# Each visit's first cast ahead of the finished visit's copies, in a grouped SwiGLU up-projection

## The chip, the cores and the metric

The kernel runs on one core of a Trainium2 chip. The metric is device time in microseconds, the median of the runs shown. A separate profiled execution gives the trace. TensorE does the matrix products; ScalarE (ACT in the profile), VectorE (DVE) and GpSimd (POOL) do the rest; SyncE (SP) issues nearly all transfers between the chip's memory and the on-chip memory. Matmul results are added up in PSUM banks.

## The reference

One decoder layer in float32, for 256 tokens and a model width of 2048:

```python
mod = (silu(c) @ w_ada + b_ada).reshape(b, 9, 2048)
h = rms_norm(x, norm_ffn1) * (1 + mod[:, 1]) + mod[:, 0]
x = x + 0.5 * mod[:, 2] * swiglu(h, w_ffn1_gu, w_ffn1_down)     # 2048 -> 2 x 5632 -> 2048
h = rms_norm(x, norm_mix) * (1 + mod[:, 4]) + mod[:, 3]
x = x + mod[:, 5] * token_mixing(h, w_in, ...)                  # retention beside windowed attention
h = rms_norm(x, norm_ffn2) * (1 + mod[:, 7]) + mod[:, 6]
x = x + 0.5 * mod[:, 8] * swiglu(h, w_ffn2_gu, w_ffn2_down)
return rms_norm(x, norm_final)

def swiglu(h, w_gu, w_down):
    gate, up = split(h @ w_gu, 2)
    return (silu(gate) * up) @ w_down
```

The change concerns the first `h @ w_ffn1_gu` alone.

## The kernel before

**Products.** Every float32 operand of a large product is split in two: a rounded high part, made by a cast on ScalarE (`split`, L374, tile `wh` for weights), and the low part, the difference, made by a subtraction on VectorE (L376, tile `wl`). Three products stand for one: high x high, low activation x high, high x low (`products`, L359). A *piece* is two blocks of 128 rows of a weight by 512 columns; for the 256 tokens (two banks) it takes 12 matmuls. Tiles `wh` and `wl` have three buffers each, so pieces can be made at most three ahead. Weights land in tiles `raw`, four buffers of 1 MB (four blocks by 512 columns).

**The grouped start.** The first up-projection begins while the conditioning vectors `mod` are still being computed from `w_ada` on VectorE (`ada_pass`, L219; its rows are loaded at L214). The 16 blocks of h therefore come in four groups of 2, 4, 6 and 4 blocks (`bounds`). For the first 8 pairs of column chunks, 16 chunks n of 512 columns (even n: gate, odd n: up), each group goes over all chunks: a *visit* is one chunk with one group's blocks, so 1, 2, 3 and 2 pieces. The order of the chunks is turned round from group to group, so that the last two chunks of a group (`stay`) are the first two of the next and keep their banks. In between, a chunk's partial sums leave PSUM: `to_parts` (L1170) copies both banks out to on-chip memory on ScalarE. PSUM has four accumulation banks here (`acc_bank`), two visits' worth. When a visit of the second or third group starts on a chunk with sums, ScalarE copies them back into its new banks (L1143), and the matmuls go on from there. The last two chunks of the third group start empty. In the fourth group (`final`) all do, and `swiglu_up` adds the kept sums on VectorE (L704, L705), then takes Silu on ScalarE (L707) and the product on VectorE (L708).

**Turning the result.** What `swiglu_up` makes is transposed by DMA: two copies on ScalarE into planes (`apart`, L534), a transpose that SyncE issues from a tile `flat` into a tile `back` (L539; `back` has four buffers), and two copies on ScalarE from `back` to their place (`together`, L550), which free the buffer. These steps are spread over later visits: `turn_step` advances every open chain (`later`) by a step, once per visit in the fourth group and once per load in the plain up-projection (`ffn_up`, `gemm_part`, loads at L350) that follows for the other three chunk pairs.

**What sets the order.** SyncE issues its transfers in the order in which the program writes them down; one that must wait, for a free buffer or for data, holds the ones behind it. On the compute engines a planner orders instructions at build time, from estimated times; at run time each engine goes through its list in that order. `tc.issue_after(ins)` ties the instructions of its block behind `ins` in the list of that instruction's engine. `cast[-1]` and `low[-1]` are the cast and the subtraction written down last. In the kernel before, the loop over the visits writes down, for one visit: its copies in, behind the cast written last; its loads; for each piece a cast, a subtraction and 12 matmuls, and in the later groups a `tick` that may write down loads and passes of conditioning rows; then in the fourth group `turn_step`; in the other groups the work for the next group's blocks of h (`coming`, with its rows); then the copies out, or `swiglu_up`.

Of the kernel before, what the change touches and what calls it, by code (L numbers as in the profile page):

```python
# [20 lines left out]
DFF = 5632  # L21
NT = S // P
KD = D // P
KF = DFF // P
CH = 512
# [52 lines left out]
def layer_kernel(  # L78
# [614 lines left out]

    def swiglu_up(banks_g, banks_u, tiles, ci, parts=None, by_dma=False):

        k0 = ci * KB
        dest = tiles[k0 // KD].rearrange("p (k s) -> p k s", s=S)
        kk = k0 % KD
        work = []
        for t in range(NT):  # L700
            s = t512()
            g, u = banks_g[t], banks_u[t]
            if parts is not None:
                nc.vector.tensor_add(s, g, parts[0][t])  # L704
# [12 lines left out]
        if work:  # L717
            turns.append(later(work))

    def ffn_up(held, w, tiles, first, bg=None, turned=(), ahead=None):  # L720
        for ci in range(first, DFF // CH):
            bg = bg or gemm(held, w, [ci * CH])[0]
            bu = gemm(held, w, [DFF + ci * CH], ahead=ahead)[0]
            swiglu_up(bg, bu, tiles, ci, by_dma=ci in turned)
            bg = ahead = None

# [326 lines left out]

    banks, moved, unlinted = {}, set(), set()
    for n, one_bank in zip(firsts, (acc_bank, side_bank)):
# [75 lines left out]

    def visit(n, ks, ends, ticks=False, ends_all=False):
        starts = n not in banks
        seeded = starts and n in moved and not ends_all
        if starts:
            banks[n] = [acc_bank() for _ in range(NT)]
        if starts:
            unlinted.discard(n)
        if seeded:
            unlinted.add(n)  # L1140
            for b, p in zip(banks[n], part_of(n)):
                with tc.issue_after(cast[-1]):
                    nc.scalar.copy(b, p)  # L1143
        raw_of = [(load_blocks(n, part), part) for part in (ks[:KB], ks[KB:]) if part]
# [4 lines left out]
        ]  # L1149
        for raw, part in pieces:  # L1150
            a, b = part[0] - ks[0], part[-1] + 1 - ks[0]
            hl = slice(part[0], part[-1] + 1)
            wh, wl = split(wsp, "w", raw[:, : len(part), :], CH)
            products(
# [4 lines left out]
                wl,  # L1159
                starts and a == 0 and not seeded,  # L1160
                b == len(ks) and ends,
                seeded=n in unlinted,
            )
            if ticks:
                tick()

    def to_parts(n):
# [16 lines left out]
    for g, ks in enumerate(groups):  # L1184
# [11 lines left out]
        for i, n in enumerate(order):  # L1196
            if g == 0 and n in firsts:
                continue
            visit(n, ks, n not in stay, g == len(groups) - 2 or final and i < 12, final or (g == len(groups) - 2 and n in stay))
            if final:  # L1200
                turn_step()
# [18 lines left out]
            elif n % 2:  # L1220
# [487 lines left out]
```

## Time and profile before

| | |
|---|---|
| median of 3 runs | 2363.13 us (2362.26 to 2363.86) |
| profiled execution, its own time | 2364.78 us |
| its span, first to last instruction | 2363.0 us |
| instructions | 28368 |
| mean granted TensorE clock | 0.999 of full speed |
| casts at L374 | 792, 1053 ns each |
| subtractions at L376 | 792, 1223 ns each |
| copies out at L1170 | 82 |
| copies in at L1143 | 52 |
| bytes read from memory | 597.16 MB, 254 GB/s over the span |

How to read the profile: times are microseconds from the first instruction of the program. PE is TensorE's matmul, PEld its weight load, which runs beside it; SPq stands for SyncE's issuing of transfers. A group or a timeline row names line, engine, operation and tiles (out<-in), a count and durations, and then the idle time of that engine just before and what ended it. A wait is put down to whatever came last. Shares of the DMA are means over 16 engines. A TensorE that is busy is not always at full rate: matmuls overlap, so the steady rate is read from the number of them in a stretch. The granted clock is a share of full speed.

### The profile page before, as it was taken

To read this page: it belongs to the slowest core of one execution; us is meant where nothing else is said; L and a number is where in the kernel's file an instruction comes from. 1 tells how busy PE (TensorE), PEld (TensorE's weight loads), DVE (VectorE), ACT (ScalarE), POOL (GpSimd) and SP (SyncE) were. 2 spreads that over 40 slices of the span, in tenths; PEclk is the share of its full clock that TensorE was granted. 3 is DMA by queue.
4 is the path that set the end of the run, shared out by engine and by line. 5 is a ranking of instruction groups with operands and counts; after the bars stand their busy time and mean duration, and the time that the engine had idled before them with its cause. 6 is when DMAs were issued, how large, how long until landed. Compare 5 with 4: busy or idle time off the path is not lost.

```text
span 2363.0 us, 28368 instructions
## 1 busy us (share of the span) xinstructions
PE 2338.4 (99%) x10447; PEld 1919.6 (81%) x10447; DVE 1670.4 (71%) x2576; ACT 1375.4 (58%) x1907; POOL 9.2 (0%) x21
## 2 busy tenths in 40 slices
PE   8999999999999999999999999999999999999998
PEld 5888788788888888778888888888888888888887
DVE  7788787778867768976777876677655555545656
ACT  6766568555556568775556554465455455455544
POOL 0000000000000000000000000000000000000000
PEclk9999999999999999999999999999999999999999
DMA  9988879988776788866688787754767777776553
GB/s 381 367 336 333 331 247 330 375 308 318 273 255 238 274 282 234 266 213 245 267 287 292 295 286 296 289 205 179 246 237 257 248 240 258 226 232 204 194 196 125
DMA packets 194765, 629.98 MB, mean 267 GB/s; under 512 B 117249, under 2 KB 117633, under 8 KB 124097
## 3 DMA queue, kind: packets, MB, share of 16 engines
q1 hardware_dynamic: 192130, 617.14, 74.5%
q0 software_dynamic: 1600, 9.83, 1.1%
q8 instruction: 82, 1.34, 0.2%
q10 hardware_dynamic: 896, 1.19, 0.1%
q14 instruction: 57, 0.47, 0.1%
HBM read 597.16 MB, written 4.22 MB: 254 GB/s over the span
## 4 chain that ended last, share of the span: by engine, by line
PE 95%; DMA 3%; ACT 1%; DVE 1%; issue 0%; SPq 0%; DVEq 0%; ACTq 0%
PE pa L359 93%; DMA raw<-in_w_ffn_gu_dram 2%; PE ps L1393 0%; ACT wh L374 0%; DMA slot<-in_w_ada_dram 0%; PE pd L1309 0%; DMA x_sb<-in_x_dram 0%; PE ps L359 0%; ACT slot L1170 0%; PE ps L893 0%; PE pd L1491 0%; PE ps L1309 0%; DVE slot L219 0%; PE pd L1492 0%; PE pd L1478 0%
## 5 line engine op out<-in xcount | busy, mean ns | idle before, releaser
L376 DVE TENSOR_TENSOR wl<-raw,wh 128x1024 fp32r<-128x1024 f32 x792 | 961.7, 1223 | 535.5 <-ACT wh L374 469.7
L374 ACT CAST wh<-raw 128x1024 fp32r<-128x1024 f32 x792 | 828.8, 1053 | 805.1 <-PE pa L359 753.7
L359 PE MATMUL pa<-wh,hh 128*128 128x512 f32 x2184 | 595.4, 392 | 7.6 <-ACT wh L374 6.9
L359 PE MATMUL pa<-wh,hl 128*128 128x512 f32 x2184 | 590.6, 390 | 0.0
L359 PE MATMUL pa<-wl,hh 128*128 128x512 f32 x2184 | 586.6, 390 | 0.0
L359 PEld LDWEIGHTS pa<-wh,hh 128*128 128x128 f32 x2184 | 407.1, 188 | 97.6 <-ACT wh L374 11.8
L359 PEld LDWEIGHTS pa<-wh,hl 128*128 128x128 f32 x2184 | 410.5, 188 | 86.3 <-issue 0.4
L359 PEld LDWEIGHTS pa<-wl,hh 128*128 128x128 f32 x2184 | 410.2, 188 | 86.4 <-issue 0.8
L359 PE MATMUL pa<-wh,a 128*128 128x512 f32 x1824 | 452.4, 389 | 0.0
L359 PEld LDWEIGHTS pa<-wh,a 128*128 128x128 f32 x1824 | 341.7, 188 | 70.5
L359 PE MATMUL pa<-wl,a 128*128 128x512 f32 x912 | 245.2, 389 | 0.0
L219 DVE CUSTOM_DVE_ANT_0 slot<-slot,cact 128x512 f32<-128x512 f32 (+2 forms) x292 | 222.2, 811 | 13.3 <-DMA slot<-in_w_ada_dram 12.9
L359 PEld LDWEIGHTS pa<-wl,a 128*128 128x128 f32 x912 | 171.1, 188 | 35.4
L550 ACT COPY slot<-back 128x512 uint16<-128x512 uint16 x156 | 104.0, 766 | 0.0
L219 DVE CUSTOM_DVE_ANT_0 rows_x<-rows_x,cact 128x512 f32<-128x512 f32 x124 | 78.8, 688 | 19.8 <-DMA rows_x<-in_w_ada_dram 19.6
L534 ACT COPY flat<-t 128x512 uint16<-128x512 uint16 x144 | 81.3, 617 | 17.1 <-DVE t L1466 5.7
L409 ACT CAST a<-slot 128x512 fp32r<-128x512 f32 x114 | 70.5, 619 | 28.6 <-PE pa L359 28.4
L410 DVE TENSOR_TENSOR a<-slot,a 128x512 fp32r<-128x512 f32 x114 | 77.9, 685 | 0.1
L219 DVE CUSTOM_DVE_ANT_0 raw<-raw,cact 128x512 f32<-128x512 f32 (+1 forms) x88 | 58.1, 712 | 14.0 <-DMA raw<-in_w_ada_dram 14.0
L1170 ACT COPY slot<-pa 128x512 f32<-128x512 f32 x72 | 38.6, 590 | 23.6 <-PE pa L359 23.5
L359 PE MATMUL pa<-wh,home 128*128 128x512 f32 x160 | 39.5, 389 | 0.0
L219 DVE DVE_READ_ACCUMULATOR2_ANT sums<- 128x1 f32 x440 | 36.4, 83 | 0.0
(223 smaller groups left out, 1079.7 us busy)
## 6 DMA issues: line engine op xcount, KB each, us to landing
raw<-in_w_ffn_gu_dram SPq DMA_DIRECT2D x160, 1024.0 KB, 5.5
raw<-in_w_in_dram SPq DMA_DIRECT2D x104, 1024.0 KB, 5.7
slot<-in_w_ada_dram SPq DMA_DIRECT2D x88, 1024.0 KB, 7.3
raw<-in_w_ffn_down_dram SPq DMA_DIRECT2D x88, 1024.0 KB, 4.9
rows_x<-in_w_ada_dram SPq DMA_DIRECT2D x31, 1024.0 KB, 7.1
raw<-in_w_ada_dram SPq DMA_DIRECT2D x21, 1024.0 KB, 5.5
raw<-in_w_swa_branch_dram SPq DMA_DIRECT2D x16, 1024.0 KB, 5.1
raw<-in_w_ret_branch_dram SPq DMA_DIRECT2D x16, 1024.0 KB, 5.4
```

The source lines that it names most:

```text
L219: nc.vector.tensor_tensor_reduce(out=w[:, at], in0=w[:, at], in1=cact[:, at], scale=1.0, scalar=0.0, op0=ALU.mult, op1=ALU.add, accum_out= ...
L359: product = nc.tensor.matmul(banks[t], act[:, j, t * P : (t + 1) * P], weights[:, j, :], start=starts and i == 0 and j == 0, stop=ends and ...
L374: cast.append(nc.scalar.copy(hi, src).ins)
L376: low.append(nc.vector.tensor_sub(lo, src, hi.bitcast(F32)).ins)
L409: nc.scalar.copy(hi, v)
L410: nc.vector.tensor_sub(lo, v, hi.bitcast(F32))
L534: nc.scalar.copy(planes[:, i, :], words(src)[:, :, i])
L550: nc.scalar.copy(into[:, :, :, i], held["turned"][:, i])
L1170: nc.scalar.copy(p, b)
```

## The change

From the second group on, once a visit's matmuls are written down, the *next* visit is begun at once: its loads, and the first of its casts and subtractions (`ready`); then, in the second and third group, its banks are opened and its sums copied in (`open_banks`). Only after that come the row loads and other work for the next group, `turn_step`, and the finished visit's copies out or its `swiglu_up`. Because `cast[-1]` now is the next visit's first cast, everything that is tied behind it (copies in, copies out, and in the fourth group the copies around the transposes) stands behind that cast. In `swiglu_up` of the grouped chunks the additions on VectorE are tied behind the next visit's first subtraction, and Silu behind its first cast. The last visit of a group begins the first visit of the next group. The last visit of the fourth group loads the first four blocks of the plain up-projection and makes its first piece (`Ahead`, `head`). The numbers of instructions and bytes stay as they are.

```diff
+    class Ahead:
+        def __init__(self, raw):
+            self.raw, self.made = raw, {}
+        def __getitem__(self, h):
+            if h not in self.made:
+                self.made[h] = split(wsp, "w", self.raw[:, 2 * h : 2 * h + 2, :], CH)
+            return self.made[h]
+
-    def swiglu_up(banks_g, banks_u, tiles, ci, parts=None, by_dma=False):
+    def swiglu_up(banks_g, banks_u, tiles, ci, parts=None, by_dma=False, behind=(None, None)):
+        def held_back(which):
+            return nullcontext() if behind[which] is None else tc.issue_after(behind[which])
...
             if parts is not None:
-                nc.vector.tensor_add(s, g, parts[0][t])
-                nc.vector.tensor_add(parts[1][t], u, parts[1][t])
+                with held_back(1):
+                    nc.vector.tensor_add(s, g, parts[0][t])
+                    nc.vector.tensor_add(parts[1][t], u, parts[1][t])
                 g, u = s, parts[1][t]
-            nc.scalar.activation(s, g, AF.Silu)
+            with held_back(0):
+                nc.scalar.activation(s, g, AF.Silu)
...
-    def ffn_up(held, w, tiles, first, bg=None, turned=(), ahead=None):
+    def ffn_up(held, w, tiles, first, bg=None, turned=(), ahead=None, head=None):
         for ci in range(first, DFF // CH):
-            bg = bg or gemm(held, w, [ci * CH])[0]
+            bg = bg or gemm(held, w, [ci * CH], ahead=head)[0]
...
-    def visit(n, ks, ends, ticks=False, ends_all=False):
-        starts = n not in banks
-        seeded = starts and n in moved and not ends_all
-        if starts:
-            banks[n] = [acc_bank() for _ in range(NT)]
-        if starts:
-            unlinted.discard(n)
-        if seeded:
-            unlinted.add(n)
-            for b, p in zip(banks[n], part_of(n)):
-                with tc.issue_after(cast[-1]):
-                    nc.scalar.copy(b, p)
+    prepared = {}
+
+    def begin(n, ks):
         raw_of = [(load_blocks(n, part), part) for part in (ks[:KB], ks[KB:]) if part]
         pieces = [...]
-        for raw, part in pieces:
+        prepared[n] = [
+            (lambda raw=raw, part=part: split(wsp, "w", raw[:, : len(part), :], CH), part)
+            for raw, part in pieces
+        ]
+
+    def ready(n, ks):
+        begin(n, ks)
+        made, part = prepared[n][0][0](), prepared[n][0][1]
+        prepared[n][0] = (lambda: made, part)
+
+    def open_banks(n, sums):
+        seeded = sums and n in moved
+        banks[n] = [acc_bank() for _ in range(NT)]
+        unlinted.discard(n)
+        fresh.add(n)
+        if seeded:
+            unlinted.add(n)
+            fresh.discard(n)
+            for b, p in zip(banks[n], part_of(n)):
+                with tc.issue_after(cast[-1]):
+                    nc.scalar.copy(b, p)
+
+    def visit(n, ks, ends, ticks=False, ends_all=False):
+        if n not in prepared:
+            begin(n, ks)
+        if n not in banks:
+            open_banks(n, not ends_all)
+        for make, part in prepared.pop(n):
...
-            wh, wl = split(wsp, "w", raw[:, : len(part), :], CH)
+            wh, wl = make()
...
             visit(n, ks, n not in stay, ...)
+            if g:
+                after = [(m, ks) for m in order[i + 1 : i + 2]]
+                if not after and not final:
+                    after = [(n, groups[g + 1])]
+                for m, ms in after:
+                    ready(m, ms)
+                    if m not in banks and not final:
+                        open_banks(m, not (g == len(groups) - 2 and m in stay))
+                if not after:
+                    head = Ahead(load(gu, 0, EARLY * CH))
+                    head[0]
             if final:
                 turn_step()
...
                 swiglu_up(..., (part_of(n - 1), part_of(n)), True,
+                    (cast[-1], low[-1]),
                 )
...
-    ffn_up(held, gu, tiles, EARLY, turned=range(EARLY, DFF // CH))
+    ffn_up(held, gu, tiles, EARLY, turned=range(EARLY, DFF // CH), head=head)
```

More of the change, by code (lines that the diff above doesn't have):

```diff
@@ L1 @@
-from contextlib import ExitStack
+from contextlib import ExitStack, nullcontext
 import numpy as np
@@ L1052, in group @@
             parts_of_h(held, k0, h)
-    banks, moved, unlinted = {}, set(), set()
+    banks, moved, unlinted, fresh = {}, set(), set(), set()
     for n, one_bank in zip(firsts, (acc_bank, side_bank)):
@@ L1159, in visit @@
                 wl,
-                starts and a == 0 and not seeded,
+                n in fresh and a == 0,
                 b == len(ks) and ends,
```

3 lines of the change are left out of this document (2 added, 1 removed).

## The prediction

> **What bounds the kernel now.** First the page's table of engines (busy time, share of the span, instructions).
>
> ```profile
> span 2363.0 us, 28368 instructions
> PE 2338.4 (99%) x10447; PEld 1919.6 (81%) x10447; DVE 1670.4 (71%) x2576; ACT 1375.4 (58%) x1907; POOL 9.2 (0%) x21
> ```
>
> TensorE is busy for 2338.4 of 2363.0 us. An edit that only orders work on ScalarE, VectorE and the SyncE queue can win what is left where it acts, no more. Where that is, stretches of the span say (start:end and length, then busy us with instruction counts of PE, PEld, DVE, ACT, POOL, then granted TensorE clock, DMA share, GB/s).
>
> ```profile
> 66.00:262.00 196.00, 195.99 (x872) 162.15 (x873) 159.13 (x251) 135.47 (x200) 0.00 (x0) 1.00 0.89 348
> 272.00:285.00 13.00, 11.06 (x42) 8.67 (x41) 9.42 (x18) 7.34 (x10) 0.00 (x0) 0.87 0.82 291
> 278.00:281.00 3.00, 3.00 (x8) 2.32 (x7) 3.00 (x7) 3.00 (x5) 0.00 (x0) 0.50 0.70 201
> 285.00:396.00 111.00, 111.00 (x491) 91.84 (x491) 93.32 (x148) 75.49 (x103) 2.10 (x4) 1.00 0.84 277
> 396.00:402.00 6.00, 5.26 (x23) 4.00 (x22) 3.00 (x4) 3.68 (x5) 0.00 (x0) 1.00 1.07 339
> 426.00:432.00 6.00, 4.30 (x20) 3.19 (x18) 3.61 (x5) 3.50 (x4) 0.00 (x0) 1.00 1.00 412
> ...
> 348.00:354.00 6.00, 6.00 (x28) 4.95 (x28) 5.23 (x8) 4.58 (x7) 0.00 (x0) 1.00 0.00 0
> ```
>
> The changed groups (second to fourth) lie between about 72 and 382 us: 111.00 us of unbroken stream hold 491 matmuls, 0.226 us each. A visit is 24 of them, 5.42 us, and 36 in the third group, 8.14 us. Until 396 TensorE is idle in one place: 13.00 - 11.06 = 1.94 us in 272:285. The clock column gives its second price: a mean of 0.87 over 13 us is 13 x 0.13 = 1.69 us lost, and 278:281 shows the clock at 0.50. Two more idle places come behind the groups, at the start of the plain up-projection: 6.00 - 5.26 = 0.74 us and 6.00 - 4.30 = 1.70 us, both at clock 1.00.
>
> What ends the first one, in time order on ScalarE and on TensorE (start, length, line, operation, count, idle time before it and what ended it), with the load that the casts read from the SyncE queue:
>
> ```profile
> 266.94 1.06 ACT L1170 COPY slot<-pa 128x512 f32<-128x512 f32 x2
> 274.88 1.07 ACT L1170 COPY slot<-pa 128x512 f32<-128x512 f32 x2 [6.88 <-PE pa L359]
> 275.83 2.00 ACT L374 CAST wh<-raw 128x1024 fp32r<-128x1024 f32 x2
> ```
> ```profile
> 276.95 1.33 PE L359 MATMUL pa<-wh,hh 128*128 128x512 f32 x4 [1.94 <-ACT wh L374]
> ```
> ```profile
> 263.75 0.86 SPq L1129 DMA_DIRECT2D raw<-in_w_ffn_gu_dram  x2
> ```
> ```profile
> raw<-in_w_ffn_gu_dram SPq DMA_DIRECT2D x2, 1024.0 KB, 7.6
> ```
>
> ScalarE stood 6.88 us in front of a copy-out (L1170) that could not run before its visit's last matmul. The next visit's first cast (L374) stood behind it. Its weights were issued at 263.75 and take 7.6 us to land (median of that stretch), so they were there by about 272, three us before. It is a matter of order on ScalarE, not of data, and it happens at one of 48 boundaries.
>
> **The change part by part.** No arithmetic is added; the instruction counts stay. These are the durations in the second and third groups (count | busy us, mean ns):
>
> ```profile
> L376 DVE TENSOR_TENSOR wl<-raw,wh 128x1024 fp32r<-128x1024 f32 x47 | 56.9, 1223 | 22.3 <-ACT wh L374 21.3 <-PE pa L359 0.8
> ...
> L374 ACT CAST wh<-raw 128x1024 fp32r<-128x1024 f32 x47 | 49.3, 1055 | 46.0 <-PE pa L359 36.9 <-DMA raw<-in_w_ffn_gu_dram 8.9
> ...
> L1143 ACT COPY pa<-slot 128x512 f32<-128x512 f32 x24 | 13.5, 602 | 0.0
> L1170 ACT COPY slot<-pa 128x512 f32<-128x512 f32 x24 | 12.8, 584 | 6.9 <-PE pa L359 6.9
> ```
>
> *First cast ahead of copy-out and copy-in.* With the edge, the cast of 1.06 us no longer follows the two copy-outs. When a visit ends, TensorE goes straight on with one piece, 12 x 0.226 = 2.71 us. In it ScalarE has two copy-outs (1.07) and the second cast (1.06): 2.13 us, so 0.58 us stay free. The low part of that second piece (1.22 on VectorE) is done 3.4 us after the boundary and first read after 2.71 + 8 x 0.226 = 4.52 us. So the stall at 275 goes and nothing follows close behind it: 1.94 idle and 1.69 of slow clock, together -3.6 us. Were the cover gone, because ScalarE's modulation work fell into the same piece, the bound would be the same stall again, 0.
>
> *Copy-in ahead of copy-out.* 0.60 us twice, early in the visit before; its banks were freed by the copy-out one visit earlier. Nothing waits: 0. What queues behind a late first cast now is the copy-in and the copy-out, and behind these the banks of the visit after next; that is 8.14 or 5.42 us ahead, and a load must be that late before it counts.
>
> *Loads on the SyncE queue.* Every visit's one or two loads (0.33 to 0.57 us of issue) move ahead of the conditioning rows that were issued between two visits, and in the fourth group ahead of the transposes. The rows then come later by one weight load at most, once, because afterwards rows and loads alternate as before. In the second and third groups TensorE does not stall on either now, so I take 0. Both ends: a row late by one 1 MB load at 348 GB/s (3 us) holds VectorE that long, and pieces are made two ahead (5.42 us), so 0 again; no gain either, since there is no second stall to remove.
>
> *Fourth group.* Here the two sides have to be worked out. The SyncE queue and ScalarE, before:
>
> ```profile
> 340.32 0.53 SPq L1129 DMA_DIRECT2D raw<-in_w_ffn_gu_dram  x1
> 353.81 1.24 SPq L539 DMA_TRANSPOSE back<-flat  x1
> 355.10 0.57 SPq L1129 DMA_DIRECT2D raw<-in_w_ffn_gu_dram  x1
> ...
> 366.81 0.53 SPq L1129 DMA_DIRECT2D raw<-in_w_ffn_gu_dram  x1
> ...
> 377.09 1.24 SPq L539 DMA_TRANSPOSE back<-flat  x1
> 378.42 0.56 SPq L350 DMA_DIRECT2D raw<-in_w_ffn_gu_dram  x1
> ```
> ```profile
> 351.42 1.06 ACT L374 CAST wh<-raw 128x1024 fp32r<-128x1024 f32 x1 [1.42 <-PE pa L359]
> 352.38 2.66 ACT L550 COPY slot<-back 128x512 uint16<-128x512 uint16 x4
> 354.91 1.03 ACT L374 CAST wh<-raw 128x1024 fp32r<-128x1024 f32 x1
> ...
> 374.70 1.05 ACT L374 CAST wh<-raw 128x1024 fp32r<-128x1024 f32 x1
> 375.66 2.66 ACT L550 COPY slot<-back 128x512 uint16<-128x512 uint16 x4
> 378.18 1.04 ACT L374 CAST wh<-raw 128x1024 fp32r<-128x1024 f32 x1
> ```
>
> A transpose waits for a free `back` buffer, that is for the copies of L550; the weight load behind it in the queue waits with it. From 340.32 to 353.81 the queue stood still, and 348:354 moved 0 GB/s. Afterwards the load of 366.81 and those behind it come just in time or late. The change does two things here. It puts the next load ahead of that transpose: the load of 355.10 goes out near 342, right behind that of 340.32 and the transpose that stood before it, into an idle stretch, and the one of 366.81 near 361 (353.81 + 3.5 of the next sentence, and what is left ahead of it: two transposes of 1.24 and a load). And it puts the copies of L550 behind the next visit's first cast instead of the last cast of the visit just done, which is one cast later: 354.91 - 351.42 = 3.5 us, and 378.18 - 374.70 = 3.5 us. The first transpose of each pair is late by that much. At the hand-over the gain stops: one `head` load comes early, but the second load of the up-projection (378.42) still follows a transpose, and so moves to about 381.9. Its flight decides:
>
> ```profile
> 378.42 6.17 DMA raw<-in_w_ffn_gu_dram
> ...
> 389.30 8.93 DMA raw<-in_w_ffn_gu_dram
> ```
>
> At 6.17 it lands at 388.1, near its due time. The second of these rows, two loads later, gave its first matmul at 389.30 + 8.93 + a cast of 1.05 = 399.3, behind 0.74 us of idle time; so TensorE reached this one at about 399.3 - 0.74 - 2 x 5.42 = 387.7, and a cast earlier is 386.7. That is 1.4 us late; if the flight is shorter, because one load was taken out of the backlog, nothing. The load of 389.30, which ends the 0.74 stall, came through full DMA engines (1.07), where the time of landing follows the volume, and the volume moved by then is the same but for what was done in the idle stretch: one load, 1 MB at the 412 GB/s of 426:432, 2.5 us (an estimate), against 3.5 us of later transposes. Ends: -2.4 us (0.74 and 1.70 both go) and +5.2 (3.5 us, and the slow clock's 1.7 with it). The two nearly cancel, so I take 0.
>
> *Gates in the fourth group.* The additions on VectorE wait for the next visit's first low part. That is done 1.06 + 1.22 = 2.3 us after the weight tile is free, one visit (5.42 us) before the banks are wanted; four banks' worth of additions behind a late load would cost the load's delay twice. At the slack above: 0.
>
> **Sum.** -3.6 + 0 + 0 + 0 + 0. Against the profiled execution's own 2364.78 us (span 2363.0 and 1.8 around it) that is 2361.2; the median of the runs, 2363.13, is 1.65 us lower, so 2359.5. About 0.2% (4.7 us) is what a measurement of this kernel can tell from no change.
>
> **A rule weighed.** The row: the clock fell to 0.50 at 278 to 281, right behind an idle time of 1.94 us, and stayed at 1.00 behind one of 1.70 us. The Trainium skill ("TensorE: Matmul & The Clock Gate", sections on what is happening and on why this matters) says that the clock drops after an idle window of about 3.4 us, so that gaps under about 3 us are safe. By that the slow clock would have another cause, and the change would win 1.94 us only. The trace does not agree, as far as one drop can say.
>
> **The rivals.**
> *B, the loads win too.* The idle stretch (0 GB/s in 348:354) gets filled, and the two later stalls go as well: 2359.5 - 2.4 = 2357.1. For it: both are ended by casts behind late loads. Against it: only one load gets ahead.
> *C, the gate costs.* The copies of L550 behind the next first cast make transposes 3.5 us late; the loads behind them keep their flights and the up-projection's start stalls 3.5 us more, passing the length at which the clock drops: +5.2 - 3.6 = +1.6, 2364.7, slower than before. It decides once the new stalls pass 3.6 us; with a drop of clock at both places (1.7 more) it is 2366.4, and with the additions held too it reaches 2368.
> *D, it does not do what it says.* Program order on ScalarE is chosen from estimated ready times. One boundary of 45 went wrong before; another may now: 2363. For it: 69% of ScalarE's time is taken in 66:262 (135.47 of 196.00), so it can find a bad place. Against: the edge excludes this very order.
> *E, the slow clock is not tied to the gap.* It recurs somewhere: 2363.1 - 1.9 = 2361.2.
>
> **How the numbers follow.** The forecast 0.40, B 0.26, C 0.15, D 0.15, E 0.04. Under 2358.4 lie nearly all of B and a quarter of the forecast's spread: faster 0.35. Over 2367.9 lie C's upper end and a little of D: slower 0.10. The rest, 0.55, is within 0.2%. The range runs from B with 1.3 us to spare, 2355.8, to C with most of a second drop of clock, 2366.0. The forecast's own is 2357.7 to 2361.3 (half of the 3.6 either way).
>
> **What would show it.** In the changed profile: the wait of copy-outs (L1170's successor) for TensorE may stay, but with a cast of the next visit in front of it; the only idle time of TensorE between 72 and 382 is gone, and the clock stays at 1.00 there; the SyncE queue issues a visit's load ahead of rows and transposes; the copies of L550 start about 3.5 us later against the matmuls; the idle times in 396:402 and 426:432 tell the forecast, B and C apart. I am wrong if a new boundary stalls, if the second load of the up-projection lands more than 4 us after its due time, or if the order behind 432 changes for the worse.

## The result, and the profile after

The changed kernel is slower: 2372.4 us (2369.76 to 2377.65, 6 runs) against 2363.27 (2362.26 to 2363.86, 6 runs) of the kernel before beside it, a ratio of 1.004 with a 95% interval of 1.0027 to 1.0053. That is 9 us where 3.6 us of gain were forecast. The profiled execution took 2371.25 us, 6.5 more than that of before. Line numbers move: loads of a visit L1129 to L1145, copies out L1170 to L1206, additions L704 to L719.

First, the stretches of the changed kernel (columns as in the prediction's first table), and TensorE's waits between 66 and 470 us (what it waited for: us in total, times, longest):

```profile
272.00:285.00 13.00, 13.00 (x59) 10.78 (x58) 11.49 (x21) 7.38 (x10) 0.00 (x0) 1.00 1.00 373
...
376.00:384.00 8.00, 6.83 (x31) 5.36 (x30) 8.00 (x21) 5.76 (x11) 0.48 (x1) 1.00 1.00 275
396.00:402.00 6.00, 0.52 (x3) 0.09 (x1) 0.00 (x0) 0.00 (x0) 0.00 (x0) 0.80 0.72 241
402.00:412.00 10.00, 5.37 (x17) 4.29 (x18) 2.36 (x2) 7.60 (x12) 0.00 (x0) 0.61 1.10 349
```
```profile
PE pa L359 <- ACT wh L374: 10.1, 1, 10.1
...
PE pa L359 <- DVE t L719: 2.0, 2, 1.2
```

The stretch 272:285 answers to the forecast's main step: 13.00 of 13.00 us busy at clock 1.00, where there were 11.06 at 0.87. ScalarE there now runs the next visit's cast ahead of the copies out:

```profile
273.25 1.05 ACT L374 CAST wh<-raw 128x1024 fp32r<-128x1024 f32 x1 [1.66 <-PE pa L359]
274.20 1.07 ACT L1206 COPY slot<-pa 128x512 f32<-128x512 f32 x2
```

Waiting, TensorE loses 10.1 us once, for a cast, and 2.0 us in two short waits for the additions. The start times of the same matmul in the two profiled executions, counted through the program, place them (worked out from the traces):

```
matmul no.   before, us   after, us   difference
  900          225.86       225.39       -0.47
 1200          297.73       293.00       -4.73
 1500          365.66       362.06       -3.60
 1600          388.32       386.16       -2.17
 1650          400.71       408.94       +8.23
 1800          437.21       443.62       +6.41
10200         2308.83      2315.21       +6.38
```

The third group gains 4.3 us. The fourth gives 1.1 of them back by matmul 1500 and 1.4 more near 380. The start of the plain up-projection, matmuls 1600 to 1650, loses 10.4. By matmul 1800 some 2.0 have come back, mostly because the wait of 1.70 us that the kernel before had at 429 is gone, and from there to the end nothing changes. The chain that ended last leads through the loss (start, length, what):

```profile
389.40 16.04 DMA raw<-in_w_ffn_gu_dram
...
405.54 1.05 ACT wh L374
...
406.63 3.58 PE pa L359 x8
```

One weight load took 16.04 us. Its counterpart before, issued at 389.30, took 8.93 and ended the wait of 0.74 us. The wait of 10.12 is thus those 0.74, 7.11 of longer flight, 2.17 by which the matmuls arrived earlier, and 0.10 of later issue. Around the load, on the SyncE queue and on GpSimd's:

```profile
388.12 1.23 SPq L539 DMA_TRANSPOSE back<-flat  x1
389.40 1.23 SPq L350 DMA_DIRECT2D raw<-in_w_ffn_gu_dram  x1
390.73 9.79 SPq L539 DMA_TRANSPOSE back<-flat  x1
400.60 1.56 SPq L350 DMA_DIRECT2D raw<-in_w_ffn_gu_dram  x1
```
```profile
388.43 0.54 POOL L305 DMA_DIRECT2D row<-gate_d  x1 [5.25 <-PE pa L359]
388.96 0.55 POOL L1309 DMA_DIRECT2D small_c<-in_consts_dram  x1
389.50 0.54 POOL L1310 DMA_DIRECT2D sink_b<-in_sinks_dram  x1
```

The prediction never counted these three GpSimd rows: the gate row `gate_load` (1 MB, one row spread over 128 partitions) and two small loads tied behind it. In the kernel before the transpose and the row were issued 1.18 us apart; now it is 0.31 us:

```profile
388.01 1.24 SPq L539 DMA_TRANSPOSE back<-flat  x1
```
```profile
389.19 0.54 POOL L305 DMA_DIRECT2D row<-gate_d  x1 [4.92 <-issue]
```

What the DMA engines did meanwhile, after (390 to 399) and before (391 to 397); the lines of the queues give packets, MB, and the time their packets took as a share of the 16 engines:

```profile
DMA packets 667, 0.69 MB, mean 76 GB/s; under 512 B 597, under 2 KB 598, under 8 KB 608
...
q1 hardware_dynamic: 592, 0.16, 58.3%
q0 software_dynamic: 75, 0.53, 55.9%
```
```profile
DMA packets 266, 2.10 MB, mean 350 GB/s; under 512 B 8, under 2 KB 8, under 8 KB 12
...
q1 hardware_dynamic: 129, 1.03, 49.8%
q0 software_dynamic: 137, 1.07, 48.9%
```

In both, SyncE's queue (q1) and GpSimd's (q0) share the engines about equally, and the engines look full. But after the change q1 carries a transpose's packets of 256 bytes in that time, and the engines move 76 GB/s instead of 350. A busy DMA share was no measure of work done.

### The profile page after: what moved, and what is told of

Its sections match the earlier page's. It is cut to its first block, busy times and chain, and to the rows that moved or that the text cites. A ratio compares the mean times of both kernels' runs of the same rounds, so it can differ in the third digit from the quotient of the medians.

```text
span 2369.4 us, 28370 instructions
## 1 busy us (share of the span) xinstructions
PE 2337.0 (99%) x10447; PEld 1918.6 (81%) x10447; DVE 1669.9 (70%) x2576; ACT 1377.8 (58%) x1907; POOL 9.2 (0%) x21
## 4 chain that ended last, share of the span: by engine, by line
PE 95%; DMA 3%; ACT 1%; DVE 1%; issue 0%; SPq 0%; DVEq 0%; ACTq 0%
PE pa L359 92%; DMA raw<-in_w_ffn_gu_dram 1%; DMA slot<-in_w_ada_dram 1%; DMA back<-flat 1%; PE ps L1441 0%; DVE slot L219 0%; ACT wh L374 0%; PE pd L1357 0%; ACT slot L550 0%; DMA x_sb<-in_x_dram 0%; DVE wl L376 0%; PE ps L359 0%; PE ps L909 0%; PE pd L1539 0%; PE ps L1357 0%
## 5 line engine op out<-in xcount | busy, mean ns | idle before, releaser
L219 DVE CUSTOM_DVE_ANT_0 slot<-slot,cact 128x512 f32<-128x512 f32 (+2 forms) x292 | 222.2, 812 | 14.0 <-DMA slot<-in_w_ada_dram 13.8
L550 ACT COPY slot<-back 128x512 uint16<-128x512 uint16 x156 | 104.0, 766 | 0.0
L219 DVE CUSTOM_DVE_ANT_0 rows_x<-rows_x,cact 128x512 f32<-128x512 f32 x124 | 78.8, 688 | 20.1 <-DMA rows_x<-in_w_ada_dram 20.0
L219 DVE CUSTOM_DVE_ANT_0 raw<-raw,cact 128x512 f32<-128x512 f32 (+1 forms) x88 | 58.1, 712 | 10.7 <-DMA raw<-in_w_ada_dram 10.5
L1206 ACT COPY slot<-pa 128x512 f32<-128x512 f32 x72 | 38.6, 589 | 11.7 <-PE pa L359 11.7
L219 DVE DVE_READ_ACCUMULATOR2_ANT sums<- 128x1 f32 x440 | 36.8, 84 | 0.0
```

What stands on the lines that cost most here:

```text
L219: nc.vector.tensor_tensor_reduce(out=w[:, at], in0=w[:, at], in1=cact[:, at], scale=1.0, scalar=0.0, op0=ALU.mult, op1=ALU.add, accum_out= ...
L550: nc.scalar.copy(into[:, :, :, i], held["turned"][:, i])
L1206: nc.scalar.copy(p, b)
```

## Where the loss comes from: four runs with a part left out

The recorded expectations name theories by number. Theory 1: the gate row's transfer and a transpose slow each other where they overlap. Theory 2: the copies tied one cast later make the loads late. Theory 3: the DMA engines are simply full there.

*Groups 2 and 3 alone.* The new order stays there; the fourth group, its ties and `head` are as before.

```diff
-            if g:
+            if g and not final:
...
-                    (cast[-1], low[-1]),
```


> The changed kernel with the new order in the second and third group only; the fourth group, its gates and the hand-over as before. The stall of 1.94 us and the slow clock near 277 go: -3.6 in all theories that lay the loss to the fourth group, so 2359.5 by theory 2. Theory 1 adds that the fourth group now runs 3.6 us earlier against the gate row, so the overlap decides: 2359.5 without one, 2365 to 2370 with one.

2360.38 us, ratio 0.9987 (0.9979 to 0.9996), 2.8 us under the kernel before. The stall at 277 is gone, the late two are 1.50 and 0.34. This part of the change wins.

*The fourth group alone.*

```diff
-            if g:
+            if final:
```


> The other half: the new order, the gates and the hand-over in the fourth group only; the second and third as before, so the stall near 277 stays (1.94 idle and 1.7 of slow clock). Theory 2: all of the loss is here, 2376. Theory 1: it depends on whether transposes meet the gate row, both of them later than in the changed kernel: 2362 without an overlap, 2370 to 2376 with one; the packets of the transposes around it tell.

2372.65, ratio 1.0044 (1.003 to 1.0058). All of the loss comes with this part. The wait in the profiled execution:

```profile
410.42 2.07 PE L359 MATMUL pa<-wh,hh 128*128 128x512 f32 x4 [11.25 <-ACT wh L374]
```

*The GpSimd loads out of the way.* The gate row, the constants and the sinks go on the SyncE queue, behind all loads of the up-projection. The same edit in the kernel before is the comparison.

```diff
-    gate_in = gate_load(gate, 2)
+    gate_load(gate, 2, nc.sync)
...
-    with tc.issue_after(gate_in.ins):
-        nc.gpsimd.dma_start(small_c[:, C_COS:], consts[:, C_COS:C_DEC])
-        nc.gpsimd.dma_start(sink_b, sinks.broadcast_to([P, QH]))
+    nc.sync.dma_start(small_c[:, C_COS:], consts[:, C_COS:C_DEC])
+    nc.sync.dma_start(sink_b, sinks.broadcast_to([P, QH]))
```


> The changed kernel, with the three loads that GpSimd's queue issues near 388 us (the gate row, spread over 128 partitions, 1 MB; 320 KB of constants; the sinks) moved to the SyncE queue behind the up-projection's loads. Theory 1 (collision): the transposes and the gate row's transfer slow each other when they overlap; without the overlap the 10.1 us stall and its slow clock (about 2 us) go: 2372.4 - 12 = 2360, and with both late stalls of before gone too perhaps 2358; transposes' packets back to a mean under 30 ns around 390. Theory 2 (the copies tied one cast later make the loads late): the stall stays, 2370 to 2372. Theory 3 (the DMA engines are simply full there): 1.4 MB less in that stretch is 3.5 us, so 2368 to 2369.

> The kernel before with the same three loads moved. Theory 1: in before the gate row's transfer starts just behind one transpose and overlaps with the next only at its end, so little is won there: the stalls of 0.74 and 1.70 us shrink or go, 2361 to 2363. Theory 3: 1.4 MB less in a stretch with full engines, both stalls go, 2360.7. Theory 2 says nothing here: 2363.

The changed kernel falls to 2363.56 (ratio to before 1.0005, 0.9997 to 1.0014), 8.8 us; the kernel before to 2360.1 (0.9988, 0.9979 to 0.9997), 3.1 us, where both late stalls go and the one at 276 stays. So three loads that the change does not touch carry most of its loss. Theory 1 had put the changed kernel at 2360; 2.8 of the 3.6 us between are what the ties cost (below). What is left in the changed kernel's waits is:

```profile
PE pa L359 <- DVE t L719: 1.1, 1, 1.1
PE pa L359 <- ACT wh L374: 0.8, 2, 0.6
```

## Volume, queue or meeting

*Same volume, same stretch, one queue.* The three loads go on the SyncE queue near 390, behind the second transpose.

```diff
-    gate_in = gate_load(gate, 2)
+    def same_volume():
+        gate_load(gate, 2, nc.sync)
+        ...                            # constants and sinks, nc.sync
+
+    ffn_up(held, gu, tiles, EARLY, ..., head=head, hook=same_volume)   # called once, behind the first chunk
```


> The changed kernel with the gate row, the constants and the sinks loaded from the SyncE queue in the stretch where GpSimd's queue loaded them: behind the second transpose near 390 us, ahead of the fifth load of the up-projection. The volume and the place are the same, but on one queue the transposes and the row's transfer follow each other. Theory 1 (overlap of two queues): no stall of 10 us; the 1.4 MB delay the loads behind them by some 3.5 us, so a stall of 0 to 3 us there, 2360 to 2364. Theory 3 (volume): the stall of about 10 us stays, 2370 to 2373.

2366.35, ratio 1.0011 (1.0002 to 1.002): 6 us of the 8.8 come back with the volume still there. The load behind the transpose took 6.39 us instead of 16.04. The time lies 2.4 us above the range that theory 1 gave; six shorter waits, 1.86 us the longest, are left. The row now lies 4.5 us later as well as on another queue, so this run alone doesn't part the two.

*Same queue, later.* In the changed kernel one element is copied into the row's tile behind a later cast, so the row must wait for it; it is issued at 397.06 instead of 388.43.

```diff
         cast.append(nc.scalar.copy(hi, src).ins)
         del cast[:-1]
+        if mark:
+            mark[1] -= 1
+            if mark[1] == 0:
+                with tc.issue_after(cast[-1]):
+                    nc.scalar.copy(mark[0][0:1, 0:1], src[0:1, 0, 0:1])
...
+    mark.extend([gate, 6])
     ffn_up(held, gu, tiles, EARLY, turned=range(EARLY, DFF // CH), head=head)
```


> The changed kernel; the gate row's load, still on the GpSimd queue, waits for a cast of the plain up-projection near 396 (a copy of one element into its tile behind that cast), so it starts some 8 us later. Same queue, same volume, same order everywhere else. Theory 1 (it harms to begin the row while a transpose's packets are under way; in the changed kernel 511 of 1024 packets were still to come when the row's first one started): the transposes near 388 and 390.5 now run alone, the stall near 406 is under 2.5 us, and the time is that of the same volume on the SyncE queue, 2366 (2364 to 2368). Rival (the changed order makes the loads late whatever the row does): a stall of 4 us or more stays, 2370 or above.

2364.5, ratio 1.0008 (0.9999 to 1.0017): 7.9 us back with the same queue and the same volume; only the row, and the two small loads tied behind it, start later. The longest wait is 1.4 us:

```profile
PE pa L359 <- ACT wh L374: 2.8, 4, 1.4
PE pa L359 <- DVE t L725: 1.9, 2, 1.0
```

The rival, an order that makes loads late whatever the row does, is out. So the queue alone is not it, and neither is the volume; it is these loads beginning while a transpose is under way.

*Not a broadcast?* The row's source becomes 127 different rows of `w_ada`; 127 of 128 partitions then lack the first block's gate.

```diff
-    gate_in = gate_load(gate, 2)
+    gate_one = nc.gpsimd.dma_start(gate[P - 1 :], gate_d[0][None, :])
+    with tc.issue_after(gate_one.ins):
+        gate_in = nc.gpsimd.dma_start(gate[: P - 1], w_ada[: P - 1, :])
```


> The changed kernel with another source for the row: 127 partitions take 127 different rows of w_ada, only one takes the gate row; so the first FFN's gate is left out in 127 of 128 partitions. Size, queue and place as in the changed kernel. If the overlap of GpSimd's queue with the transposes is what costs, whatever is read, the long stall stays: 2368 to 2374, transposes' packets of several hundred ns. If it is that 128 partitions read the same 8 KB, it goes: 2360 to 2364.

2367.86 (1.002, 1.001 to 1.0029), just under the first expectation, with a stall of 5.67 us. The 127 rows were issued 0.24 us later than the row in the changed kernel, behind the single row's load, and their first packet came 2.6 us behind the issue instead of 2.0. So the meeting itself moved, and only 25 of the transpose's packets were left. The 127 rows' own packets took 612 ns in the mean. The run tells little on the broadcast, only that other rows harm too.

*Elsewhere in the kernel before.* The same copy of one element holds the row behind its sixth, seventh and eighth cast of the plain up-projection (2.3, 5.8 and 9.5 us later).

```diff
+    mark.extend([gate, 6])     # 7, 8
     ffn_up(held, gu, tiles, EARLY, turned=range(EARLY, DFF // CH))
```


> The kernel before; the gate row's load on the GpSimd queue waits for the sixth cast of the plain up-projection (near 391.1), by a copy of one element into its tile behind that cast, so it starts about 3.3 us later. No volume is added and nothing else is moved. Theory 1 (the row's transfer and transposes slow one another when they are under way together): the first packet comes near 394.4, with transposes due at 394 to 396; if 100 or more of their packets are then to come, the row takes 8 us or more instead of 6.3 and the kernel is slower by 3 to 10 us (2366 to 2373); if it meets none, 2363 +- 1. Rival (only the volume on the DMA engines counts, wherever it lies): 2363 +- 1 even where they meet.

> As the run before, with the row's load behind the seventh cast (near 398.3, its first packet near 401.5). There the transposes are through or not yet begun (their packets lie near 398 to 400 and 404 to 406 in the kernel before). Theory 1: only the end of the row meets transposes, so the loss is small, 2363 to 2365, and the stall of 0.74 at 398 goes since the load before it has the engines for itself. Rival (volume only): 2363 +- 1 as well; this run gives the row without the meeting, for comparison with the other two.

> As the two runs before, behind the eighth cast (near 399.3, first packet near 402.4 and the row under way to about 406), so that the transposes' packets of 404 to 406 fall into it. Theory 1: transposes' packets in the row's window are many and slow, over 50 ns in the mean, the row takes 8 us or more, the kernel is slower by 3 to 10 us. Rival (volume only): 2363 +- 1. If the meeting is there and the row still moves at 300 GB/s or more, theory 1 needs a second condition, which would then be sought in the start of the two (the row begun while a transpose is half through, as in the changed kernel).

2362.14 (0.9997, 0.9987 to 1.0006), 2362.64 (0.9998, 0.9989 to 1.0007) and 2364.36 (1.0001, 0.9992 to 1.0011). None met a transpose: none was under way when the row began, at most 42 packets of the next one fell into the row's time, at 18 ns each, and the row's packets took 314 ns. They show the row harmless elsewhere, not the meeting.

*The row twice.* In the kernel before the row is loaded a second time.

```diff
+    gate_load(gate, 2)
     gate_in = gate_load(gate, 2)
```


> The kernel before with its gate row loaded a second time on the GpSimd queue, behind the first load and the two small ones: 1 MB more, which should run into the transposes that the kernel before issues near 401.7. Nothing of the order on ScalarE, VectorE or SyncE is changed. Theory 1 (a row transfer on the GpSimd queue and transposes on the SyncE queue slow one another): the transposes near 401.7 take 8 us or more to land where they took 3 to 4, and the kernel is 5 to 10 us slower, 2368 to 2373. Rival (only the volume counts, 1 MB at the rate of this stretch): +2.8 us, 2366.0, with the transposes' landing time hardly changed. If the second load misses the transposes, the second number says nothing against the first theory.

2365.48, ratio 1.001 (1.0001 to 1.0019). The row issued second, ahead of the small loads, found no transpose under way (400.69 to 404.47, 314 ns a packet) and cost 2.5 us, about what 1 MB takes at the 412 GB/s of the prediction's row 426:432 (an estimate).

*Bringing the meeting about in the kernel before.* One copy on ScalarE ahead of the copies of L550 makes the transpose later.

```diff
         def together():
+            if mark:
+                to, of = mark.pop()
+                with tc.issue_after(cast[-1]):
+                    nc.scalar.copy(to, of)          # 128x768, or 128x512
             with tc.issue_after(cast[-1]):
```


> The kernel before; one copy of 128x768 is put on ScalarE in front of the copies of L550 near 386.6, which free the buffer for the transpose near 388.0. It takes some 0.85 us, so that transpose is issued at about 388.9, 0.3 us ahead of the row's load at 389.19, as in the changed kernel (0.31); before, it was 1.18. Nothing else changes; the copy's own result is written over. Theory 1: the row's first packet (near 391.05) finds some hundred packets of the transpose still to come; the transposes take 8 us or more to land, TensorE stalls 4 to 11 us behind the next load, and the kernel is slower by 3 to 10 us, 2366 to 2373. Rival (the changed order of loads, casts and gates is what costs, the meeting only goes with it): 2363 +- 1.

> As the run before, with a copy of 128x512, some 0.6 us: the transpose near 388.6, 0.6 us ahead of the row's load. Theory 1: fewer packets are still to come when the row begins, 0 to 300, and the loss is between nothing and that of the longer copy, 2363 to 2369. Rival: 2363 +- 1.

2364.48 (1.001, 1.0001 to 1.0019) and 2363.37 (1.0002, 0.9993 to 1.0011). The transposes were issued 0.54 and 0.74 us ahead of the row; only 28 and 46 of 1024 packets were left when the row began. TensorE's wait behind the next load rose from 0.74 to 2.04 and 2.35 us, of which 0.61 and 1.14 are longer flight; the rest is that the copy made the load itself later against the matmuls:

```profile
398.27 1.88 PE L359 MATMUL pa<-wh,hh 128*128 128x512 f32 x4 [2.04 <-ACT wh L374]
```
```profile
400.14 2.00 PE L359 MATMUL pa<-wh,hh 128*128 128x512 f32 x4 [2.35 <-ACT wh L374]
```

I did not reach the full meeting there, and the times stay under the 2366 that theory 1 gave the longer copy at least. Put side by side, one profiled execution each, sorted by how much of the transpose was left (packets counted in the traces):

```
                                 transpose packets   the load behind it   TensorE's wait
                                 left at the row's   took to land, us     for that load, us
                                 first packet
changed, row later                      0                  6.20               0.24
kernel before                           0                  8.93               0.74
before, row twice                       6                  9.84               1.58
groups 2 and 3 alone                    7                  9.70               1.50
before, copy of 128x768                28                  9.54               2.04
before, copy of 128x512                46                 10.07               2.35
changed, no ties (below)              107                 11.17               4.38
changed                               511                 16.04              10.12
fourth group alone                    511                 17.27              11.25
```

With 107 and 511 packets left the load is clearly slower; up to 46 its flights of 8.93 to 10.07 us don't follow the count. The run with other source rows falls outside the series (25 left, 11.67, 5.67), and that of 107 packets was an execution 2.5 us faster than its kernel's median. That the meeting causes most of the 10 us rests on the run that takes it away from the changed kernel, and on the upper end of this series.

It had been close before: the transpose's last packet started at 390.81, the row's first at 391.05, 0.24 us later. The change made the row's data ready earlier (row issued at 388.43 instead of 389.19) and the transpose 0.1 us later. It took one thing more. In the kernel before all 1024 packets of that transpose took 0.96 us; at that pace they would have been through at 390.24 in the changed kernel, 0.22 us ahead of the row's first packet at 390.46. But there a packet of 16 KB of instructions (queue q8) started at 389.16, just ahead of the transpose's first at 389.29, and half of the packets alone took 1.14 us. This goes with the order of the loads: in all nine runs with the new order of the fourth group's loads the q8 packet starts within 0.2 us of that transpose's first packet, and the transpose takes 2.2 to 2.6 us even in the five where no row is near; in the eight runs with the old order it starts at the transpose's end, and the transpose takes 0.94 to 0.96 us. In the two runs with the added copy it falls inside the transpose, which takes 2.4 and 2.7. That the q8 packet slows the transpose is not shown by an edit of its own. Without the row it did no harm: with the loads moved it started at 388.87, and the time was 2363.56.

## What the ties and the earlier loads do

*No ties in* `swiglu_up`, first with the three loads on the SyncE queue, then with the row still on GpSimd's.

```diff
-                    (cast[-1], low[-1]),
```


> The changed kernel with the three loads moved behind the up-projection's loads, and without the two ties in swiglu_up (additions behind the next first low part, Silu behind the next first cast). With the ties the changed kernel with moved loads is at 2363.6 and shows idle times of 0.28 and 1.09 us near 335 and 380, the second ended by an addition on VectorE. If the ties make them: both go, -1.4 to -2, 2361.6 to 2362.2. If it is the late loads in front of the additions: no change, 2363.6.

> The changed kernel without the two ties in `swiglu_up` (the additions behind the next low part, Silu behind the next cast); the gate row stays on the GpSimd queue. Without the GpSimd loads in the way these ties cost 2.8 us. Theory 1 (the gate row's transfer on the GpSimd queue runs at the same time as the transposes and slows them): the row waits on work that the ties do not order, so the long stall of TensorE near 406 stays and the time falls by the ties' 2.8 us alone, 2369.6 (2367 to 2371). Rival (the ties hold the chunk's result back, so that its transposes come late enough to meet the gate row): the overlap goes with the ties, the stall near 406 is under 3 us, and the time is about 2363.

2360.72 (0.9989, 0.9981 to 0.9998): 2.8 us less than with the ties, more than the 1.4 to 2 expected, and the waits at 335 and 380 go. With the row on GpSimd's queue 2366.78 (1.0019, 1.001 to 1.0028), between the two expectations: 5.6 us less. The ties cost their 2.8, and they also place the meeting (107 packets left instead of 511 in the profiled executions); that this makes the other 2.8 is an inference. The ties' cost stands in VectorE's rows of the changed kernel:

```profile
375.51 0.69 DVE L219 CUSTOM_DVE_ANT_0 slot<-slot,cact 128x512 f32<-128x512 f32 x1 [2.57 <-DMA slot<-in_w_ada_dram]
...
377.96 1.22 DVE L376 TENSOR_TENSOR wl<-raw,wh 128x1024 fp32r<-128x1024 f32 x1
379.10 1.28 DVE L719 TENSOR_TENSOR t<-pa,a 128x512 f32<-128x512 f32 x2
```
```profile
379.93 0.70 PE L359 MATMUL pa<-wh,hh 128*128 128x512 f32 x2 [1.17 <-DVE t L719]
```

Four conditioning passes (L219) that had waited for a row stood in front of the subtraction, the additions were tied behind it, and the banks came free 1.17 us late.

*Loads early, cast not.* The kernel before with the three loads moved, and each visit's loads written down ahead of the finished visit's copies, as are the copies in of the second and third group; no cast is made ahead, and there are no ties in `swiglu_up`.

```diff
     def ready(n, ks):
         begin(n, ks)
-        made, part = prepared[n][0][0](), prepared[n][0][1]
-        prepared[n][0] = (lambda: made, part)
...
-                    head[0]
...
-                    (cast[-1], low[-1]),
```


> The kernel before with the gate row and the two small loads on the SyncE queue (2360.1), and of the change one part alone: each visit's loads are written down before the finished visit's copies and copies in, but its first cast is not made ahead. Theory (the stall of 1.94 us at 275 is ScalarE's order, a first cast behind a copy-out that waits for TensorE): the stall stays or another boundary stalls in its place, and the time is 2360.1 +- 1; the version with the cast ahead in the second and third group, and the same loads moved, had 2357.9. Rival (the gain came from the earlier loads): the stall is gone and the time is 2357.9 or below. In the fourth group the earlier load may cost or win up to 2.5 us at the start of the plain up-projection; the profile's idle times at 275 and behind 395 tell the two apart.

2359.85 (0.9988, 0.998 to 0.9997), the time that my theory gave, but the stall at 275 is gone, against it. ScalarE's rows say why:

```profile
274.11 1.05 ACT L374 CAST wh<-raw 128x1024 fp32r<-128x1024 f32 x1 [1.67 <-PE pa L359]
275.07 1.07 ACT L1204 COPY slot<-pa 128x512 f32<-128x512 f32 x2
```

It is still the order on ScalarE: the cast runs ahead of the copy-out. But no tie to that cast is needed; with the loads and the copies in written down earlier the planner puts it there; which of the two does it was not tried. Two waits of 0.72 and 1.14 us remain behind.

*What wins.* The new order in groups 2 and 3 alone, and the three loads on the SyncE queue.

> The new order in the second and third group only, and the three loads of GpSimd's queue moved behind the up-projection's loads on the SyncE queue. The two gains add if they are independent: 2363.2 - 2.8 - 3.1 = 2357.3; no idle time of TensorE over 0.5 us between 72 and 450 us.

2357.9, ratio 0.9977 (0.9968 to 0.9987): faster than both kernels. TensorE does not wait in the whole stretch:

```profile
72.00:440.00 368.00, 368.00 (x1632) 304.20 (x1631) 301.34 (x491) 252.44 (x356) 0.48 (x1) 1.00 0.89 332
```

From the changed kernel to this one, by medians: 2372.4, row later 2364.5, the three loads out of the stretch 2363.56, ties away 2360.72, the rest of the fourth group's order away 2357.9. Each comparison with before is good to about 2 us, so the steps of 2.8 are sure in sign by the profile's waits more than by the times; of the last, 1.3 us are short waits between 382 and 524, and the rest stays open.

## Why the prediction was wrong

*First cast ahead of the copies: right.* Forecast -3.6; the stall goes as described, matmuls 900 to 1200 gain 4.3 us, and groups 2 and 3 alone win 2.8. The size was a bit high: of its 1.69 us of slow clock not every execution has a share (below).

*Copies in ahead, and loads ahead of rows: 0, right.* TensorE did not wait at any boundary of the second and third groups.

*Fourth group, "The two nearly cancel, so I take 0": this step failed.* The sum itself did not cancel: 2.5 us against 3.5, and ends of -2.4 and +5.2, leave a loss of 1.0 to 1.4. Of its parts, the copies of L550 did come later against the matmuls, by about 2.3 us at 386.7, where 3.5 was worked out (their start is 0.1 later, the matmuls are 2.2 earlier). The second load of the up-projection did not move to 381.9: it went out at 377.80, the third at 379.75, and no stall came there. What failed is the flight of the load that came at 389.30 before. I took 6.17 to 8.93 us from rows, and argued that with full engines "the time of landing follows the volume". It took 16.04, 7.11 more than before, with engines as full as before and 76 GB/s. Behind it is an omission: I counted the SyncE queue and never GpSimd's, which carries a megabyte in the very stretch I was pricing. A GpSimd timeline of 380 to 400 would have shown the row 1.18 us behind a transpose that I had just worked out to come 3.5 us later.

*Gates: 0, wrong.* 0.85 and 1.17 us of waits, 2.8 us by the medians. This step failed too. The reasoning gave a visit (5.42 us) of room, but counted from the time the weight tile was free, not from VectorE's list, where conditioning passes may stand ahead of the subtraction.

*The rivals.* C had the sign and the place (a load behind a transpose made late, the clock down after it), but it let the loads "keep their flights", so its price ended at 3.5 us a load and 2368 in all; it came nearest to the time, but not by the cause. Of B's two late stalls the second went; the first is the one that grew to 10.12 us. D's new bad place on ScalarE did not appear. E's rule is answered below. The signs that I named (idle times in 396:402, a late load) did find the cause at once.

## What to carry to other kernels

When an edit moves transfers of one queue, list what every other queue has under way in that stretch, GpSimd's lone loads too, and the gap between each pair: a gap of 0.24 us is a condition, not a margin. A DMA share near 1 is not throughput; read the GB/s beside it. And a tie costs what stands ahead of its anchor in that engine's list, so price it from a timeline and not from the anchor's own duration.

## What the runs showed of the hardware

*Transposes and another queue's transfer.* Apart, a transpose's 256-byte packet took 18 ns (kernel before, near 390) and the row's 8 KB one 314 ns (the runs with the row later). In the changed kernel's window (390.46 to 401.41) 532 transpose packets took 156 ns in the mean, 147 of them over 100 ns, the row's packets 773 ns, and the whole moved at 144 GB/s. With the row on the SyncE queue the load behind the transpose took 6.39 us. What inside the DMA engines does this is open. The Trainium skill ("DMA: Bandwidth & Descriptors", rules for kernel authors) says that a transpose beside ordinary transfers needs nothing; that is about order and data, and for the time these runs do not agree.

*The clock behind an idle TensorE.* In the profiled executions of all 19 kernels, between 66 and 1200 us, none of 22 idle times of 0.74 to 1.70 us was followed by a lower clock; all five of 2.35 to 11.25 were; of 13 between 1.86 and 2.07, 8 were. What decides shows in the clock's own times. In all 19 executions the clock changes between full and half only at whole multiples of 3.413 us, counted from its first rise: in the kernel before it rises at 21.85, falls at 277.85 (75 steps) and is back at 281.27 (76). The two idle times of one execution, that of the kernel before with the copy of 128x768, laid into these steps:

```profile
272.23:275.64 3.41, 1.92 (x9) 1.26 (x7) 0.40 (x4) 1.63 (x3) 0.00 (x0) 1.00 0.94 334
275.64:279.05 3.41, 2.97 (x13) 2.46 (x14) 2.99 (x5) 3.41 (x6) 0.00 (x0) 1.00 0.84 345
...
395.11:398.52 3.41, 1.37 (x6) 0.83 (x6) 0.38 (x2) 1.35 (x2) 0.00 (x0) 1.00 1.03 321
398.52:401.93 3.41, 3.41 (x9) 2.63 (x9) 2.09 (x2) 3.41 (x6) 0.00 (x0) 0.50 1.02 423
```

The idle 1.94 us are split over two steps, 1.49 and 0.44, and the clock stays at 1.00. The 2.04 us lie in one step, and the next one runs at 0.50. So it is with all nine executions that have the 1.94 us: the three that kept the clock have them split, the six that lost it have them in one step. Over all 19, of 19 steps with 1.86 us or more of idle TensorE 18 were followed by a step at half clock; of the steps with 1.65 us or less it was one, whose own clock was already half; the two between, 1.76 and 1.79, went one each way. So the slow clock is tied to the gap, as the forecast had it against rival E, and for gaps of some 2 us it hangs on where the gap falls. The Trainium skill ("TensorE: Matmul & The Clock Gate", section on what is actually happening) speaks of a free-running window of about 3.4 us, and the trace agrees (3.413 us). The Trainium skill also advises (same page, section on why this matters) to allow no idle gaps over about 3 us; here a gap of 1.86 us was enough.
